# A decoder block on one core: earlier copies in the Entries, a reordered head, and attention keys split one step later

## The chip, the cores and the metric

One Trainium2 chip, one of its cores. The metric is the device time of one execution in microseconds; three runs of the kernel before are known, and one further execution was profiled.

## The reference

A hybrid decoder block on one sequence of 1024 tokens, model width 1024, in float32:

```python
h = x + 0.5 * swiglu(rms_norm(x, g1), w1a, w3a, w2a)           # swiglu: (silu(x@w1) * (x@w3)) @ w2, width 2816
u = rms_norm(h, g_mix)
q, k, v, p, gates = split(u @ w_in)                            # 768, 768, 768, 512, 2 x 1024 columns
y_attn = dilated_mixture_attention(q, k, v) @ w_branch_attn    # 3 groups of 4 heads, dilations 1, 4, 16, partial rotary
y_pool = multiscale_pool(p, pool_w, pool_scale) @ w_branch_pool
h = h + (sigmoid(gA) * y_attn + sigmoid(gB) * y_pool) @ w_out
h = h + 0.5 * swiglu(rms_norm(h, g2), w1b, w3b, w2b)
out = rms_norm(h, g_final)
```

## The kernel before, in words

Every large product is done in float32 by three matmuls of the format fp32r: each operand is split into an upper part (hi, a rounded copy made by ScalarE) and a lower part (lo, the operand minus hi, made by VectorE or GpSimd), and hi·hi, hi·lo and lo·hi are added up in PSUM. On top of that, products of 1024 x 1024 blocks go by a scheme of seven half-size products instead of eight (numbered 1 to 7, order 1, 6, 2, 7, 5, 4, 3), for which both operands need sums and differences of their quarters. TensorE, its weight loads, VectorE (DVE), ScalarE (ACT), GpSimd (POOL) and the DMA queues (most issued by SP, some by ACT) each work through their own queue in the order in which the program issues; most of that order is written out by hand (`manual_schedule`).

The stages, with the times in the profile at which they run:

- **Head** (0 to 28 us, `begin_up1`). Loads x and the gain, takes the squares and inverse roots of the first four row tiles (`squares` on ACT, `inverse` on DVE and then POOL), scales them, transposes them on TensorE (`Rows`) and makes their hi and lo. `keep_on` issues idle matmuls. The first four products (`entry.product(0)` to `(3)`) stand between.
- **Entry** (class `Entry`; three times: 28 to 60 us, 665 to 696 us, 1282 to 1315 us). While the first products of the stage run, it prepares the last four row tiles t = 4 to 7. Step t issues product i, three sets of transposes (y's high half for b22, all of it for t1 = its low half minus b11, and t3), product k = i + 1, and around them the sums t1, t2, t4 (on DVE, in PSUM), their hi on ACT, their lo on DVE, the weights two products ahead (`operand`: hi on ACT, lo on POOL or DVE), the outputs (`out`) and the scaling of the next tile. Product 2 of a quarter scheme accumulates in the bank of product 1, so it must wait until the output of product 1 has been copied out. `more` asks for the weights that the stage needs after the Entry; with `early` it only makes their sums s1 and s2 (`Quad.summed(6)`). `high(t, 0)` is `inverse(t)`, `high(t, 1)` the scaling, `after(t)` squares of tile t + 2 and loads. The four PSUM banks called "acc" are used in turn: the last transposes of step 7 take the bank that the lower part of t4 of step 6 has read last.
- **Up** (to 448 us, and from 1315 to 1713 us): the seven products for each pair of blocks of w1 and w3.
- **Down** (448 to 665 us, 1713 us to the end; class `Down`): steps of 24 matmuls; `begin(i + 2)` splits the operands of the step after next. Of the left operand's lower parts every second one goes to POOL in two halves, the others to DVE.
- **Mix** (696 to 1053 us): the input projection, with jobs between: rotations (`Mix.rotate`: y is stored, its rotary rows are gathered by DMA into a tile `ro`, turned, and stored), values transposed, pooling, late weights split. A job's `yield n` says that it goes on n products later.
- **Attention** (1053 to about 1180 us): 24 steps q of two slots of 128 queries each. Step q issues the scores of its slots, the transposes of the exponents of q - 1, branch products as filling, the values of q - 2, masks on DVE, and then on ACT the hi of the transposed exponents, the hi of the next head pair's keys and queries (`split_ring`, lo on POOL) and the exponents of step q.
- **Merge and output projection** (1180 to 1282 us): `merge(k)` on all engines, then 14 steps (`step_o`) of the seven-product scheme with left operands split by `split_o`; `rows_first2`, `lower` and `scaled2` prepare the second Entry between its last steps.

## Time and profile before

| | us |
|---|---|
| median of 3 runs | 1932.86 (1932.31 to 1933.2) |
| the profiled execution | 1933.69 |
| its span, first to last instruction | 1931.8 |
| TensorE busy (matmul) | 1900.9 |
| VectorE busy | 1341.1 |
| ScalarE busy | 776.9 |
| GpSimd busy | 732.4 |

Rows of the profile name the engine, the line of the kernel, the operation, and `out<-in` by the tiles' names (`u_f12a`: a product of the first up stage, pair 2, matrix a; `wc`: a split weight; `xhi`, `xlo`: parts of x; `alo`, `blo`: lower parts in a down stage; `tp`: transposed exponents). In a timeline the first number is the start in us, the second the duration, and square brackets tell how long the engine had been idle and what ended that. A matmul row counts as busy while it is in the pipeline, at a lowered clock too. The granted clock is given by the windows view as a share of full speed.

### The profile page before, as it was taken

Reading aid. Unit: us, or ns where it says so; the run is one execution under the profiler, and the core shown is the slowest. Engines: PE = TensorE matmul, PEld = TensorE weight load, DVE = VectorE, ACT = ScalarE, POOL = GpSimd, SP = SyncE. Lnnn points to the kernel's source line nnn. Section 1 sums busy time; section 2 is a strip of 40 time slices with the busy share of each in tenths; the row PEclk is TensorE's granted clock in tenths of the full one; section 3 lists DMA queues with packets and bytes.
Section 4 is the critical chain, followed back from the end, with each engine's and each line's share of the span. In section 5 each row is a group of like instructions: output and inputs, shape, how many; then the busy total and the mean of one; then the engine's idle time right before and its main releaser. Section 6 shows DMA issues by size and latency. Waiting matters only on the chain. (4 is left out here: it accounts for less than half of the span.)

```text
span 1931.8 us, 24861 instructions
## 1 busy us (share of the span) xinstructions
PE 1900.9 (98%) x8842; PEld 1567.5 (81%) x8842; DVE 1341.1 (69%) x2012; ACT 776.9 (40%) x1397; POOL 732.4 (38%) x559
## 2 busy tenths in 40 slices
PE   9999999999999999999999999999999999999998
PEld 7788888888888877888877888877888888888886
DVE  6786556658676776667775796877666556577777
ACT  6333333333345542334435663263323333333344
POOL 4333333332222344444545365543333333322133
PEclk9999999999999999999999999999999999999999
DMA  4154222336466637764568997643533223454564
GB/s 187 44 196 167 90 88 104 136 115 212 145 237 206 201 93 230 232 234 180 208 248 307 269 240 263 246 167 99 190 104 136 82 87 107 150 193 139 195 213 164
DMA packets 147436, 333.56 MB, mean 173 GB/s; under 512 B 20208, under 2 KB 40944, under 8 KB 145776
## 3 DMA queue, kind: packets, MB, share of 16 engines
q1 hardware_dynamic: 138096, 307.22, 47.1%
q10 hardware_dynamic: 9216, 24.75, 3.7%
q8 instruction: 70, 1.15, 0.2%
q14 instruction: 54, 0.44, 0.1%
HBM read 229.61 MB, written 102.30 MB: 172 GB/s over the span
## 5 line engine op out<-in xcount | busy, mean ns | idle before, releaser
L768 PE MATMUL d_f<-bhi_f,alo_f 128*128 128x512 f32 x616 | 240.4, 390 | 1.6 <-POOL alo_f L730 1.2
L768 PE MATMUL d_f<-bhi_f,ahi_f 128*128 128x512 f32 x616 | 240.6, 391 | 1.2 <-ACT ahi_f L726 0.7
L768 PE MATMUL d_f<-blo_f,ahi_f 128*128 128x512 f32 x616 | 239.8, 389 | 0.0
L730 POOL TENSOR_TENSOR alo_f<-g_f,ahi_f 128x512 fp32r<-128x512 f32 x68 | 96.9, 1442 | 278.6 <-ACT ahi_f L726 278.6
L314 PE MATMUL u_mixm<-xhi_t_mix,wc_mixm 128*128 128x512 f32 x608 | 195.2, 392 | 1.1 <-POOL wc_mixm L306 1.1
L314 PE MATMUL u_mixm<-xhi_b_mix,wc_mixm 128*128 128x512 f32 x456 | 148.8, 393 | 3.9 <-DVE y_m L1051 2.0
L768 PEld LDWEIGHTS d_f<-bhi_f,alo_f 128*128 128x128 f32 x616 | 115.6, 188 | 27.8 <-POOL alo_f L730 2.3
L768 PEld LDWEIGHTS d_f<-bhi_f,ahi_f 128*128 128x128 f32 x616 | 115.6, 188 | 25.6 <-ACT ahi_f L726 1.2
L314 PEld LDWEIGHTS u_mixm<-xhi_t_mix,wc_mixm 128*128 128x128 f32 x608 | 113.7, 188 | 26.4 <-POOL wc_mixm L306 3.0
L768 PEld LDWEIGHTS d_f<-blo_f,ahi_f 128*128 128x128 f32 x616 | 115.7, 188 | 23.9 <-DVE blo_f L730 0.2
L314 PE MATMUL u_mixm<-xlo_t_mix,wc_mixm 128*128 128x512 f32 x304 | 118.4, 389 | 0.0
L306 POOL TENSOR_TENSOR wc_mixm<-s_mixm,wc_mixm 128x512 fp32r<-128x512 f32 x52 | 75.2, 1447 | 102.8 <-ACT wc_mixm L303 87.9
L314 PEld LDWEIGHTS u_mixm<-xhi_b_mix,wc_mixm 128*128 128x128 f32 x456 | 85.6, 188 | 23.4 <-ACT late_hi L1194 2.6
L303 ACT ACTIVATE wc_mixm<-s_mixm 128x512 fp32r<-128x512 f32 x76 | 47.7, 629 | 124.8 <-DVE s_mixm L353 53.4
L314 PE MATMUL u_mixm<-xlo_b_mix,wc_mixm 128*128 128x512 f32 x228 | 88.8, 389 | 0.0
L726 ACT ACTIVATE ahi_f<-g_f 128x1024 fp32r<-128x1024 f32 x84 | 81.8, 974 | 3.0 <-DMA g_f<-gs_f 3.0
L306 POOL TENSOR_TENSOR wc_mixm<-raw,wc_mixm 128x512 fp32r<-128x512 f32 x40 | 56.5, 1414 | 59.1 <-ACT wc_mixm L303 56.5
L1958 PE MATMUL wo<-w_o,o_hi 128*128 128x512 f32 x224 | 69.5, 391 | 0.5 <-ACT h_again L395 0.3
L726 ACT ACTIVATE bhi_f<-s_f2w 128x512 fp32r<-128x512 f32 x55 | 32.9, 628 | 89.0 <-DVE s_f2w L746 81.3
L314 PEld LDWEIGHTS u_mixm<-xlo_t_mix,wc_mixm 128*128 128x128 f32 x304 | 57.1, 188 | 11.8
L726 ACT ACTIVATE bhi_f<-s_f1w 128x512 fp32r<-128x512 f32 x55 | 33.0, 630 | 79.4 <-DVE s_f1w L746 74.6
L730 DVE TENSOR_TENSOR alo_f<-g_f,ahi_f 128x1024 fp32r<-128x1024 f32 (+1 forms) x44 | 52.7, 1197 | 7.2 <-ACT ahi_f L726 7.2
(1332 smaller groups left out, 5099.8 us busy)
## 6 DMA issues: line engine op xcount, KB each, us to landing
g_f<-gs_f SPq DMA_DIRECT2D x70, 512.0 KB, 4.5
gs_f<-y_f SPq DMA_DIRECT2D x88, 256.0 KB, 2.5
raw<-in_w2a_dram SPq DMA_DIRECT2D x35, 512.0 KB, 3.9
raw<-in_w2b_dram SPq DMA_DIRECT2D x35, 512.0 KB, 4.1
gs_f<-gb_f SPq DMA_DIRECT2D x46, 256.0 KB, 2.3
raw<-in_w1a_dram SPq DMA_DIRECT2D x22, 512.0 KB, 4.7
raw<-in_w3a_dram SPq DMA_DIRECT2D x22, 512.0 KB, 5.8
raw<-in_w1b_dram SPq DMA_DIRECT2D x22, 512.0 KB, 4.6
```

The costliest lines, as they stand in the source:

```text
L303: ac.activation(w[:, 0], src, AF.Copy)
L306: eng.tensor_tensor(w[:, 1], src, w[:, 0].bitcast(F32), op=OP.subtract)
L314: pe.matmul(p, a, b, start=(start and k == 0 and q == 0), stop=(k == 3 and q == 2), skip_group_check=not start)
L726: ac.activation(hi[:, c], src, AF.Copy)
L730: eng.tensor_tensor(lo[:, d], src[:, o], hi[:, d].bitcast(F32), op=OP.subtract)
L768: pe.matmul(self.banks[m][t], l, r, start=(first and q == 0), stop=(last and q == 2))
L1958: pe.matmul(banks[m][t], l, r, start=(st == 0 and j == 0 and q == 0), stop=(st == 1 and j == 1 and q == 2))
```

## The change

It has these parts; nothing else of the kernel differs, and every engine does the same arithmetic, apart from what moves between engines.

- Entries: the output of product i is issued right behind the first upper part, and no longer behind all three; the squares of the tile after next (`after`) come before the fourth part; the inverse of a tile is issued at the end of the step two before it; the next tile is scaled before the weights of product k + 2 are split; of the weight sums, s1 is made in step 5 and s2 in step 6, and the weight they belong to is split behind the lower part of t4.
- Head: the identity is loaded first; the squares of tiles 1 to 3 are issued in a row, the four lower parts behind the four scalings; the high half of the gain is copied by ACT and no longer by DVE; product 0 goes by terms (4 x hi·hi, 4 x with w's lower part, 4 x with x's).
- Down stages: the lower part of the left operand of step 1 is made by DVE in one piece, not by POOL in two.
- Rotations: the gathering of the rotary rows is issued one product later, and one multiplication moves from POOL to DVE.
- Attention: the next head pair's keys and queries are split in steps 3 and 4 for the first use, not in steps 2 and 3.
- Output projection: the first left operand is split by halves, and `scaled2(3)` is issued behind the first two lower parts.

The diff:

```diff
@@ -294,6 +294,7 @@
         def __init__(self, name, X, fw, fs=None):
             self.name, self.X, self.fw, self.fs = name, X, fw, fs or fw
             self.n_lo = 0
+            self.by_term = False
 
         def half_tile(self, tag, n):
             return self.fs.tile([P, HALF], F32, tag=tag, bufs=4, name=f"{tag}_{self.name}{n}")
@@ -308,11 +309,13 @@
 
         def product(self, p, w, x, start=True):
             hi, lo = self.X[x]
-            for k in range(4):
+            order = [(k, q) for k in range(4) for q in range(3)]
+            if self.by_term:
+                order = [(k, q) for q in (0, 2, 1) for k in range(4)]
+            for n, (k, q) in enumerate(order):
                 r = slice(k * P, (k + 1) * P)
-                for q, (a, b) in enumerate(three((w[:, 0, r], w[:, 1, r]), (hi[:, k, :], lo[:, k, :]))):
-                    pe.matmul(p, a, b, start=(start and k == 0 and q == 0), stop=(k == 3 and q == 2),
-                              skip_group_check=not start)
+                a, b = three((w[:, 0, r], w[:, 1, r]), (hi[:, k, :], lo[:, k, :]))[q]
+                pe.matmul(p, a, b, start=(start and n == 0), stop=(n == 11), skip_group_check=not start)
 
     ORDER = (1, 6, 2, 7, 5, 4, 3)
 
@@ -323,6 +326,7 @@
             self.sv, self.n = sv, n
             self.a = []
             self.bank, self.w, self.src = {}, {}, {}
+            self.s1 = None
 
         def get(self):
             r = raws.get()
@@ -332,7 +336,7 @@
             self.summed(m)
             self.w[m] = self.sv.split(self.src.pop(m), f"{self.n}{m}", eng)
 
-        def summed(self, m):
+        def summed(self, m, whole=True):
             if m in self.src:
                 return
             if not self.a or (m not in (1, 2) and len(self.a) == 2):
@@ -347,8 +351,11 @@
             elif m == 4:
                 src = a22
             elif m == 6:
-                self.s1 = half_tile("s", f"{n}1")
-                ve.tensor_tensor(self.s1, a21, a22, op=OP.add)
+                if self.s1 is None:
+                    self.s1 = half_tile("s", f"{n}1")
+                    ve.tensor_tensor(self.s1, a21, a22, op=OP.add)
+                if not whole:
+                    return
                 self.s2 = half_tile("s", f"{n}2")
                 ve.tensor_tensor(self.s2, self.s1, a11, op=OP.subtract)
                 src = self.s2
@@ -451,11 +458,13 @@
                     ve.tensor_tensor(t2, t2, b21, op=OP.subtract)
                     return Parts(X, "t4", t2, t)
 
+                if t == 4:
+                    high(5, 0)
                 self.product(i)
                 if not last:
-                    high(t + 1, 0)
                     self.operand(i + 2)
                     s = Rows(X, "b22", y[:, HIGHS], t)
+                    self.out(i)
                 else:
                     r3 = Rows(X, "t3", t3, t)
                 p12 = bank("acc", f"x_b12_{t}")
@@ -469,18 +478,22 @@
                     t2 = bank("acc", f"x_t2_{t}")
                     s.lower()
                     r1.lower()
-                    self.out(i)
                     self.product(k)
+                    y, t3 = scaled_rows(t + 1)
                     self.operand(k + 2)
-                    y, t3 = scaled_rows(t + 1)
                     r2 = second()
                     r3.lower()
                     r2.lower()
                     self.out(k)
+                    after(t)
                     r4 = fourth()
+                    if t > 4:
+                        self.more(0, t - 4)
+                    r4.lower()
                     if t == NT - 2:
                         self.more(0)
-                    r4.lower()
+                    if t + 2 < NT:
+                        high(t + 2, 0)
                 else:
                     t2 = bank("acc", f"x_t2_{t}")
                     r2 = second()
@@ -497,9 +510,7 @@
                     s.lower()
                     r4.lower()
                     self.out(k)
-                after(t)
-                if t == NT - 3:
-                    self.more(0, True)
+                    after(t)
 
 
     class Pair:
@@ -718,7 +729,7 @@
             )
             self.n_lo += 1
             whole = len(srcs) == 1 and srcs[0].shape[1] > 1
-            eng = gp if self.n_lo % 4 == 0 and n < len(self.steps) - 2 else ve
+            eng = gp if self.n_lo % 4 == 0 and 1 < n < len(self.steps) - 2 else ve
             at = 0
             for src in srcs:
                 n = src.shape[1]
@@ -817,6 +828,7 @@
     warm = consts.tile([P, 1], F32, name="warm")
     cnt = consts.tile([P, 4, 16], F32, name="cnt")
     psc = consts.tile([P, 4], F32, name="psc")
+    nc.scalar.dma_start(ident, c_ident)
     nc.scalar.dma_start(gain1, ffn1_norm)
     ac.activation(warm, mhalf, AF.Silu)
 
@@ -836,7 +848,6 @@
     columns = columns_tile.rearrange("p (k c) -> p k c", k=KT)
 
     def load_all():
-        nc.scalar.dma_start(ident, c_ident)
         load_rows(0, 1, 2, 3)
         raws.depth = 2
         raws.load()
@@ -852,7 +863,7 @@
 
     def pre_run(sv, todo, first, low):
         return Entry(sv, [(*((q.A, m, q.a_out), (q.B, m, q.b_out))[k],) for q, m in todo for k in range(2)], low,
-                     lambda n, early=False: (first.A.summed if early else first.A.operand)((6, 7)[n]))
+                     lambda n, part=0: first.A.summed(6, part > 1) if part else first.A.operand((6, 7)[n]))
 
     def begin_up1():
 
@@ -890,30 +901,29 @@
         g = [gains(b) for b in range(2)]
         keep_on(2)
         ve.tensor_copy(gain_row[:, LOWS], g[0])
-        squares(1, square)
-        squares(2, square)
+        for t in range(1, 4):
+            squares(t, square)
         rows(0, "b11", LOWS)
         inverse(1)
         keep_on(2)
+        rows(1, "b11", LOWS)
         inverse(2)
-        squares(3, square)
-        rows(1, "b11", LOWS)
-        r[0].lower()
-        keep_on(3)
+        keep_on(2)
         rows(2, "b11", LOWS)
         inverse(3)
-        r[1].lower()
         keep_on(3)
         pairs = [Pair(sv1, j, sums, True, j == 2) for j in range(3)]
         entry = pre_run(sv1, [(q, m) for m in (1, 2) for q in pairs[:2]] + [(pairs[2], m) for m in (1, 2)],
                         pairs[0], h[:4])
         entry.operand(0)
         rows(3, "b11", LOWS, "mm")
-        r[2].lower()
         keep_on(2)
-        r[3].lower()
-        ve.tensor_copy(gain_row[:, HIGHS], g[1])
+        ac.activation(gain_row[:, HIGHS], g[1], AF.Copy)
+        for t in range(4):
+            r[t].lower()
+        sv1.by_term = True
         entry.product(0)
+        sv1.by_term = False
         entry.operand(1)
         for t in range(4):
             r[t].keep(h[t][:, LOWS])
@@ -1085,14 +1095,14 @@
                     nc.scalar.dma_start(given[:, a, n].rearrange("t r c -> r t c"),
                                         y[a][n * HD:n * HD + 16].rearrange("r (t c) -> r t c", t=2))
                 nc.scalar.dma_start(qk_dram[u][a].rearrange("h d c -> (h d) c"), y[a])
-                yield 1 + a
+                yield 1 + 2 * a
             ro = tmp(f"ro{u}").rearrange("p (a c) -> p a c", a=2)
             nc.scalar.dma_start(ro[:, 0, :], given.rearrange("t a h r c -> (t a h r) c"))
             yield 3
             tab = tables[g]
 
             ve.stream_shuffle(ro[:, 1, :], ro[:, 0, :], [i ^ 8 for i in range(32)])
-            gp.tensor_tensor(ro[:, 1, :], ro[:, 1, :], tab[:, 1, :], op=OP.mult)
+            ve.tensor_tensor(ro[:, 1, :], ro[:, 1, :], tab[:, 1, :], op=OP.mult)
             ve.tensor_tensor(ro[:, 0, :], ro[:, 0, :], tab[:, 0, :], op=OP.mult)
             if self.hp == 1 and g + 1 < GROUPS:
                 load_table(g + 1)
@@ -1264,13 +1274,13 @@
     mixes = [Mix(svm, q) for q in range(AHEAD)]
     items = [(q, m) for q in range(len(MIX)) for m in ORDER if q >= AHEAD or m not in (1, 2)]
 
-    def mix_operand(k, early=False):
+    def mix_operand(k, part=0):
         if k < len(items):
             q, m = items[k]
             if q == len(mixes):
                 mixes.append(Mix(svm, q))
-            if early:
-                mixes[q].quad.summed(m)
+            if part:
+                mixes[q].quad.summed(m, part > 1)
             else:
                 mixes[q].quad.operand(m, None if k > 1 else gp)
 
@@ -1845,9 +1855,12 @@
                 load_ring(uses[u + 1], ring_place(u + 1))
             if q > 0:
                 advance(splits[q - 1], 2)
-            if i > 1 and u + 1 < len(uses):
+            if i > 1 and 0 < u < len(uses) - 1:
                 split_ring(uses[u + 1], i - 2)
                 split_ring(uses[u + 1], i)
+            if q in (3, 4):
+                split_ring(uses[1], q - 3)
+                split_ring(uses[1], q - 1)
             end_branches()
             exponents(2 * q)
             exponents(2 * q + 1)
@@ -1936,8 +1949,11 @@
             for q in range(2):
                 gp.tensor_tensor(lefts[i][:, q], srcs[0][:, q], srcs[1][:, q], op=left[2])
 
+    def o_parts(i):
+        return tuple(op.tile([P, 2, HALF], F32R, tag=f"a{part}", bufs=3, name=f"o_{part}{i}") for part in ("hi", "lo"))
+
     def hi_o(i):
-        ops[i] = tuple(op.tile([P, 2, HALF], F32R, tag=f"a{part}", bufs=3, name=f"o_{part}{i}") for part in ("hi", "lo"))
+        ops[i] = o_parts(i)
         ac.activation(ops[i][0], lefts[i], AF.Copy)
 
     def lo_o(i):
@@ -1945,6 +1961,13 @@
         ve.tensor_tensor(lo, lefts.pop(i), hi.bitcast(F32), op=OP.subtract)
 
     def split_o(i):
+        if i == 0:
+            ops[i] = o_parts(i)
+            (hi, lo), src = ops[i], lefts.pop(i)
+            for q in range(2):
+                ac.activation(hi[:, q], src[:, q], AF.Copy)
+                ve.tensor_tensor(lo[:, q], src[:, q], hi[:, q].bitcast(F32), op=OP.subtract)
+            return
         hi_o(i)
         lo_o(i)
 
@@ -2044,7 +2067,6 @@
         scaled2(1)
         inverse(3)
         scaled2(2)
-        scaled2(3)
         step_o(STEPS - 4)
         raws.end = len(raws.pieces)
         raws.depth = 4
@@ -2052,6 +2074,7 @@
         r = [rows_first2(t) for t in range(2)]
         step_o(STEPS - 3, range(2))
         lower(0, r[0])
+        scaled2(3)
         lower(1, r[1])
         split_o(STEPS - 1)
         r.append(rows_first2(2))
```

## The prediction

> **What bounds the kernel now.** The page comes first: the span, and the share of each engine.
>
> ```profile
> span 1931.8 us, 24861 instructions
> ...
> PE 1900.9 (98%) x8842; PEld 1567.5 (81%) x8842; DVE 1341.1 (69%) x2012; ACT 776.9 (40%) x1397; POOL 732.4 (38%) x559
> ```
>
> TensorE is busy for 98% of the span, so nothing can be won by taking work off another engine as such. The change adds no matmul and removes none; it can only shorten TensorE's waits. The second view lists those waits by who ended them (microseconds in total, times, longest).
>
> ```profile
> PE tp L1630 <- ACT e L1610: 2.6, 2, 2.5
> PE u_f12a L314 <- ACT y_f L535: 2.3, 1, 2.3
> PE u_f21a L314 <- ACT y_f L535: 2.3, 1, 2.3
> PE u_mixm L314 <- DVE y_m L1051: 2.0, 3, 1.3
> PE u_mixm L314 <- ACT y_m L1040: 1.9, 1, 1.9
> PE d_f L768 <- POOL alo_f L730: 1.2, 2, 0.6
> PE x_b L387 <- DVE x L270: 1.1, 3, 0.6
> ...
> PE wo L1958 <- DVE o_lo L1945: 0.5, 1, 0.5
> ...
> PE u_f10a L314 <- DVE xlo_b_f L391: 0.2, 1, 0.2
> ```
>
> These rows come to 14.1 us. Rows 2, 3 and 5 are the three Entries, row 1 the start of attention, row 4 the mix stage beside a rotation, row 6 the two down stages, row 8 the first output step, rows 7 and 9 the head. Every edit aims at one of them. A wait can cost more than it lasts, which the third view shows: TensorE's busy time, then its granted clock, over windows of 3.41 us.
>
> ```profile
> 684.26:687.67 3.41, 1.86 (x9) 1.00 0.00 0
> 1066.55:1069.96 3.41, 0.90 (x10) 1.00 0.88 258
> 1302.07:1305.48 3.41, 1.06 (x5) 1.00 0.00 0
> 52.79:56.20 3.41, 3.41 (x9) 0.50 0.45 154
> 1069.96:1073.38 3.42, 3.42 (x13) 0.50 1.05 377
> 1305.48:1308.90 3.42, 3.42 (x9) 0.50 0.38 147
> ```
>
> After each of the three waits of over 2.3 us TensorE runs one stretch of 3.41 us at clock 0.50, counted as busy. It does half the work of that stretch, so each of these waits costs a further 3.41 / 2 = 1.71 us. The 1.9 us wait (first row, 45% idle) costs none; the two windows with 69 and 74% idle do. The Trainium skill (TensorE: Matmul & The Clock Gate, "What's actually happening") says the clock falls to half only after a whole idle window of about 3.4 us; by it none of these waits could do this, and the 5.1 us would not be among the gains. The trace agrees on the half clock and the window's length, but windows 69% idle are enough here, and I go by the trace.
>
> **The Entries.** Step t of an Entry does two products with three sets of transposes between; VectorE takes the sums and lower parts. In the second Entry (last: products of f21a and f21b), timeline rows of VectorE, ScalarE, TensorE:
>
> ```profile
> 1300.84 0.69 DVE L407 TENSOR_TENSOR xlo_t_f<-x_t,xhi_t_f 128x512 fp32r<-128x512 f32 x1 [0.66 <-ACT xhi_t_f L404]
> 1301.44 0.68 DVE L351 TENSOR_TENSOR s_f20a<-raw 128x512 f32<-128x512 f32 x1
> 1302.16 0.69 DVE L353 TENSOR_TENSOR s_f20a<-s_f20a,raw 128x512 f32<-128x512 f32 x1
> 1302.77 0.15 DVE L263 TENSOR_SCALAR nst<-nst 128x1 f32<-128x1 f32 x1
> ...
> 1309.95 0.69 DVE L306 TENSOR_TENSOR wc_f20a<-s_f20a,wc_f20a 128x512 fp32r<-128x512 f32 x1 [1.18 <-ACT wc_f20a L303]
> 1310.56 0.68 DVE L407 TENSOR_TENSOR xlo_t_f<-x_t,xhi_t_f 128x512 fp32r<-128x512 f32 x1
> ```
>
> ```profile
> 1301.22 0.59 ACT L388 ACTIVATE xhi_b_f<-x_b 128x512 fp32r<-128x512 f32 x1
> ...
> 1304.53 0.60 ACT L535 ACTIVATE y_f<-u_f21a 128x512 f32<-128x512 f32 x1
> ```
>
> ```profile
> 1305.18 0.56 PE L314 MATMUL u_f21a<-xhi_b_f,wc_f21a 128*128 128x512 f32 x1 [2.35 <-ACT y_f L535]
> ...
> 1311.30 0.66 PE L387 MATMUL x_b<-ident,hn_f 128*128 128x128 f32 x4 [0.63 <-DVE xlo_t_f L407]
> 1311.71 0.47 PE L314 MATMUL u_f21b<-xhi_b_f,wc_f21b 128*128 128x512 f32 x1
> ```
>
> The product at 1305.18 accumulates in the bank that the copy at 1304.53 must first read. That copy stands on ScalarE behind two upper parts, and one of these behind VectorE's queue with the two weight sums. The change puts the copy (out) right behind the upper part at 1301.22, which needs no sum: it then ends at about 1301.22 + 2 x 0.6 = 1302.4, before TensorE comes at 1305.18 - 2.35 = 1302.83. So the 2.35 us and, with it, the 1.71 us go.
>
> What is late next is VectorE. The last step's third set of transposes (1311.30) needs the bank freed by the lower part at 1310.56. On the path to it: the two weight sums, 1302.77 - 1301.44 = 1.33 us, now fill waits of 0.66 such as the one at 1300.84 (one a step earlier, one in step 6), and the weight's lower part at 1309.95 moves behind the lower part. Of its wait and pitch, 1.18 + 0.61 = 1.79 us, 0.66 stays as the wait for the upper part, so 1.1 us goes. The squares, moved ahead of the fourth part, free ScalarE sooner for the next step's first upper part, of which I count 0.3; the copy now stands ahead of t1's upper part and of VectorE's lower part that needs it, at most 0.6, of which I count 0.25. Sum 1.33 + 1.1 + 0.3 - 0.25 = 2.5 us; TensorE arrives sooner than that and waits about 2 us in two pieces in the last step. I take 2.4 (bounds 0, if the new waits bring the slow clock and a late operand, to 2.35 + 1.71 + 0.63 = 4.7).
>
> The first Entry has the same sums, but its weight's lower part is POOL's, so the 1.1 is missing: 1.33 + 0.3 - 0.25 = 1.4, more where the slow products had been the later of the two; with the head below, 2.0 (bounds 0.5 to 4.1). The mix Entry likewise: 1.4 (bounds 0.5 to 1.9 + 0.3). The weight loads that follow the squares on SP's queue go out with them, sooner and waited for by nobody here. On POOL the subtraction for t3 now stands ahead of the second weight's lower part; both are wanted within one product, which hides the later one (if not: up to 0.7 us in a step, in the bounds).
>
> **Head.** Squares in a row, lower parts all behind the four scalings, and the first product by terms: it needs its x lower parts only for its last four matmuls. Against that, each scaling now follows its own inverse through POOL, with no lower part between to fill VectorE, and ident's load, first on ScalarE's queue, puts gain1 one issue later. The two waits rows of the head hold 1.3 us; I take 0.3 (bounds -0.6 to 0.6), inside the 2.0 above.
>
> **Down stages.** Step 1's left lower part goes from POOL (two halves) to VectorE (one).
>
> ```profile
> 443.55 3.48 DVE L730 TENSOR_TENSOR blo_f<-s_f1w,bhi_f 128x512 fp32r<-128x512 f32 x2
> 446.95 1.21 DVE L730 TENSOR_TENSOR alo_f<-g_f,ahi_f 128x1024 fp32r<-128x1024 f32 x1
> ...
> 449.41 1.28 DVE L730 TENSOR_TENSOR blo_f<-s_f1w,bhi_f 128x512 fp32r<-128x512 f32 x2
> ```
>
> ```profile
> 443.08 3.39 POOL L730 TENSOR_TENSOR alo_f<-g_f,ahi_f 128x512 fp32r<-128x512 f32 x2 [2.90 <-ACT ahi_f L726]
> ```
>
> Beside POOL's 3.39 us the two VectorE ops take 3.48; alone, at 449.41, 1.28. Queued behind them are the pair's last outputs and step 2's sums. So 2.2 us is won and the new op costs 1.2: VectorE runs about 1.0 us ahead. The 0.6 us wait comes two steps later, at step 3, whose lower part stays on POOL; it is fed through VectorE's sums and shrinks by about 0.5, and step 0's own lower part, at 446.95, is sooner. Taken: 0.6 for each of two stages, 1.2 (bounds 0 to 1.5).
>
> **Rotations.**
>
> ```profile
> 731.13 1.78 DVE L351 TENSOR_TENSOR s_mixm<-raw 128x512 f32<-128x512 f32 x1
> ...
> 735.03 0.68 DVE L1051 TENSOR_TENSOR y_m<-u_mixm,y_m 128x512 f32<-128x512 f32 x1
> ```
>
> The 1.3 us wait ends with the op at 735.03, late because the shuffle, a multiplication and two weight sums stand before it, one of them stretched to 1.78 beside POOL's multiplication. One step later the shuffle and both multiplications stand behind it, and the reload on ScalarE's queue no longer holds up the engine until its own store has landed (a second of the three waits, all on L1051). 2.0 us is listed; I take 1.6 (bounds -1 to 2.0).
>
> **Attention.**
>
> ```profile
> 1068.07 0.63 ACT L1221 ACTIVATE xlo_b_mix<-xhi_b_mix 128x512 fp32r<-128x512 f32 x1 [2.10 <-DMA xhi_b_mix<-rot]
> ```
>
> ```profile
> 1068.78 1.27 POOL L1222 TENSOR_TENSOR xhi_b_mix<-xhi_b_mix,xlo_b_mix 128x512 fp32r<-128x512 f32 x1 [1.45 <-ACT xlo_b_mix L1221]
> ```
>
> ```profile
> 1069.25 2.17 PE L1630 MATMUL tp<-ident,e 128*128 128x128 f32 x8 [2.46 <-ACT e L1610]
> ...
> 1074.65 0.33 PE L1583 MATMUL s<-xlo_b_mix 64*128 64x128 f32 x2
> ```
>
> ```profile
> 1369.92 19.04 PE u_f22a L314 x84
> ```
>
> ScalarE stands in its queue for a load that lands at 1068.07, with the exponents behind it. A step later it does not. TensorE then goes on at 1069.25 - 2.46 = 1066.79 with 8 transposes (half of 2.17, which was at half clock), 4 matmuls (19.04 / 84 = 0.227 each, the last row, from the chain) and the values (12 of half that width, 1.4), and reaches the next scores, at 1074.65 now, at 1070.2. But these need the second lower part: ScalarE makes ehi from about 1067.4 and the ring's upper parts from 1068.6 (four copies of 0.6), POOL two lower parts of 1.27 from 1069.25, the second done at 1071.8. A new wait of about 1.4 us, too short for the slow clock: gain 1074.65 + 0.16 - 1071.85 = 2.9, taken as 2.7 (bounds 1.5 to 2.46 + 1.71 = 4.2).
>
> **Output steps.**
>
> ```profile
> 1187.51 0.50 PE L1958 MATMUL wo<-w_o,o_lo 128*128 128x512 f32 x1 [0.53 <-DVE o_lo L1945]
> ```
>
> By halves, the first lower part is ready before TensorE comes: the 0.53, a shorter wait just before it, and the restarts around both: 1.0 (bounds 0.5 to 1.2). On VectorE the second half waits for its upper part with the next merge's multiplication behind it, as the whole does now. scaled2(3), moved behind the first lowers, frees two banks sooner, but the next rows wait for copies queued behind an unmoved split: 0 (bounds -0.2 to 0.4).
>
> **Sum.** 2.0 + 1.4 + 2.4 + 1.2 + 1.6 + 2.7 + 1.0 = 12.3 us. The profiled execution took 1933.69, so 1921.4; the median of the three runs, 1932.86, is 0.83 below it, so 1920.6.
>
> **Rivals.**
> The slow clock stays in two Entries: the new waits there (about 2 us in one window of 3.41, 59% idle) lie between the 45% that did no harm and the 69% that did. 2 x 1.71 = 3.4 us back: 1924.0. Chance 0.20.
> The three slow stretches have another cause than the waits and stay: 3 x 1.71 = 5.1 us, 1925.7. All three follow the three longest waits, so 0.04. The Trainium skill's rule above would have it so.
> VectorE is no bound: the Entries' waits go whole, 4.1 + 1.9 + 4.7 instead of 5.8, 4.9 us more: 1915.7. Chance 0.10.
> Slower: VectorE's share of a rotation (a shuffle and two multiplications, of 0.7 us each like the sum at 1301.44, or up to 1.78 each beside POOL's other ops) now delays an output that a product waits for, six times. If each of the six costs over 12.3 / 6 = 2.05 us the change loses; at 2.35 + 1.71 = 4.06 us each it is 24.4 us, 1945.0. Against it: the trace shows one long wait of this kind among six rotations. Chance 0.07.
> The edits only move waits, and nothing is gained: 1932.9. Chance 0.03.
>
> **How the numbers follow.** The forecast has the remaining 0.56. The range 1915.5 to 1926.5 holds it and the first three rivals (0.90), with the bounds inside each. Faster 0.90, same 0.03, slower 0.07; 0.2%, 3.9 us, is about what a measurement of this kernel can tell from no change.
>
> **What would show it.** In the profile after: no wait of u_f12a, u_f21a and u_mixm for ACT y; a wait of x_b for xlo_t of 1 to 2 us in each Entry; a wait of s for POOL's ring of about 1.4 us near 1070; clock 1.00 throughout; no wait over 0.3 us for POOL alo_f at step 3; wo's first lower part without a wait. I am wrong if a window of an Entry shows clock 0.50, if rotations show waits over 2 us, or if the exponents still wait for the load.

## The result, and the profile after

The change makes the kernel faster: 1923.76 us median of 4 executions (1921.17 to 1925.59) beside 1933.03 before; the ratio is 0.9951, with a 95% interval of 0.9934 to 0.9968. The forecast was 1920.6, with a range of 1915.5 to 1926.5. The profiled execution of the changed kernel took 1924.18 us.

The page of the changed kernel, span and engines:

```profile
span 1922.4 us, 24860 instructions
...
PE 1896.7 (99%) x8840; PEld 1566.1 (81%) x8840; DVE 1337.6 (70%) x2020; ACT 777.4 (40%) x1399; POOL 715.8 (37%) x549
```

TensorE's work is the same; the span is 9.4 us shorter. The waits of TensorE by who ended them (microseconds in total, times, longest):

```profile
PE x_b L394 <- DVE xlo_t_f L414: 3.2, 2, 1.6
PE yp L1727 <- DMA wab<-late_w: 1.7, 1, 1.7
PE x_b L394 <- DVE xlo_t_mix L414: 1.6, 1, 1.6
...
PE wo L1981 <- ACT h_again L402: 1.0, 1, 1.0
...
PE wo L1981 <- DVE o_lo L1961: 0.8, 1, 0.8
...
PE d_f L779 <- POOL alo_f L741: 0.6, 2, 0.3
PE u_mixm L318 <- DVE y_m L1061: 0.6, 2, 0.3
```

All five long waits of before are gone: the copies of the three Entries, the exponents, and the 1.3 us one beside a rotation. Rows 1 and 3 are the forecast's wait of TensorE for VectorE, 1.6 us in the last step of each Entry. Row 2 was not forecast: attention now waits for a branch weight's load, where a wait for POOL's part of the keys had been expected. Rows 4 and 5 are the output stage, where the wait of 0.53 us shrank to 0.23 and longer ones came later.

The windows view (TensorE busy and its count, weight loads, VectorE, ScalarE, POOL, then the granted clock, DMA share, GB/s):

```profile
1297.21:1300.62 3.41, 1.73 (x13) 1.07 (x12) 3.23 (x6) 2.35 (x5) 1.74 (x2) 1.00 0.48 159
1300.62:1304.04 3.42, 3.42 (x11) 2.84 (x11) 3.35 (x6) 2.39 (x5) 0.00 (x0) 0.50 0.45 143
1061.69:1065.11 3.42, 1.76 (x11) 1.51 (x11) 2.10 (x8) 3.42 (x11) 1.98 (x2) 1.00 1.03 388
```

One stretch at clock 0.50 is left, where three were: it follows a window of the second Entry that was 49% idle (1 - 1.73 / 3.41). The third row, 49% idle too by the rounded numbers (1 - 1.76 / 3.42), has no slow stretch behind it.

Where the 9.4 us came from is read from the timeline of TensorE: the start of the first matmul of a stage, in both kernels, and the difference from one such start to the next (the head from the start of the span, the last stage to the end of its last matmul). For the second Entry and the products behind it, the timeline of the changed kernel:

```profile
1274.30 0.39 PE L318 MATMUL u_f20a<-xhi_b_f,wc_f20a 128*128 128x512 f32 x1
...
1703.23 0.39 PE L779 MATMUL d_f<-bhi_f,ahi_f 128*128 128x512 f32 x1
```

and of the kernel before:

```profile
1282.06 0.39 PE L314 MATMUL u_f20a<-xhi_b_f,wc_f20a 128*128 128x512 f32 x1
...
1712.48 0.39 PE L768 MATMUL d_f<-bhi_f,ahi_f 128*128 128x512 f32 x1
```

That is 428.93 against 430.42 us, 1.5 less. So for all stages, in the profiled executions:

| stage (from its first matmul to the next stage's) | before, us | after, us | gain | forecast |
|---|---|---|---|---|
| head, to the first transposes of t3 in the first Entry | 31.97 | 32.84 | -0.9 | 0.3 |
| first Entry and its products | 415.49 | 413.16 | 2.3 | 1.7 |
| first down stage | 217.89 | 216.86 | 1.0 | 0.6 |
| mix Entry, to its first product of t2 | 30.91 | 28.98 | 1.9 | 1.4 |
| rest of the mix stage, rotations | 356.86 | 355.26 | 1.6 | 1.6 |
| attention, to its last product of values | 118.15 | 116.06 | 2.1 | 2.7 |
| merge and output projection | 110.79 | 111.14 | -0.4 | 1.0 |
| second Entry and its products | 430.42 | 428.93 | 1.5 | 2.4 |
| second down stage | 212.64 | 212.47 | 0.2 | 0.6 |

The same table was made for each run below; it says more than the total, because some stages repeat within a few hundredths where no slow stretch (3.41 us at clock 0.50) falls and no load is late: the second Entry's stage took 427.55 to 427.59 us in seven kernels that have the changed Entry, or one that differs from it only in its last step, and no slow stretch in it. The head (31.97 to 32.70 with its old code), the rest of the mix stage (355.92 to 356.86) and the second down stage (212.46 to 212.82) scatter more, so one trace decides nothing there that is smaller. Attention took 117.15 to 118.87 us in the four kernels with its old code and no idle matmuls, a slow stretch in each.

### The profile page after: what moved, and what is told of

Same layout as the page of the kernel before. It is cut to its first block, busy times and chain, and to the rows that moved or that the text cites. A ratio compares the mean times of both kernels' runs of the same rounds, so it can differ in the third digit from the quotient of the medians.

```text
span 1922.4 us, 24860 instructions
## 1 busy us (share of the span) xinstructions
PE 1896.7 (99%) x8840; PEld 1566.1 (81%) x8840; DVE 1337.6 (70%) x2020; ACT 777.4 (40%) x1399; POOL 715.8 (37%) x549
## 5 line engine op out<-in xcount | busy, mean ns | idle before, releaser
L741 POOL TENSOR_TENSOR alo_f<-g_f,ahi_f 128x512 fp32r<-128x512 f32 x64 | 90.1, 1426 | 284.1 <-ACT ahi_f L737 275.8
```

What stands on the lines that cost most here:

```text
L741: eng.tensor_tensor(lo[:, d], src[:, o], hi[:, d].bitcast(F32), op=OP.subtract)
```

## The experiments

The theory was that VectorE's queue sets the end of each Entry, that half-idle windows bring the half clock, and that each part gains what its stage's next operand allows. Each run's before is the median beside which it was timed.

**Idle matmuls in the long waits of the kernel before.** Seven matmuls of ones go into a bank that is written next:

```diff
+                if last:
+                    b7 = bank("acc", f"x_t3_{t}")
+                    for _ in range(7):
+                        pe.matmul(b7[:, :P], ones, ones, start=True, stop=True)
                 self.product(i)
...
+        for _ in range(7 if q == 3 else 0):
+            pe.matmul(banks[0][:, :P], ones, ones, start=True, stop=True)
```

> The kernel before with seven matmuls of ones, whose result nobody reads, ahead of the last step's first product in each Entry and ahead of the transposes of the exponents of step 3 of attention, so that TensorE is busy in the three waits of over 2.3 us, which stay as long as they are. My theory (these waits bring the half clock): the three stretches at clock 0.50 vanish and nothing else changes, 3 x 1.71 = 5.1 us, 1932.9 - 5.1 = 1927.8. Rival (the slow stretches have another cause): they stay, no change, 1932.9. If idle matmuls themselves are late for the waiting operations: up to 0.3 us each slower.

Measured: 1935.79 (1934.25 to 1936.81), before 1933.41; ratio 1.0011 (1.0001 to 1.0020). The clock stayed at 1.00 in both Entries of its trace, so the waits do bring the half clock there. In the second Entry the idle matmuls waited 1.4 us for their own bank and filled the rest. In attention they ran too soon, the transposes waited 3.2 us behind them, and the slow stretch came twice: that stage took 121.53 us instead of 118.15, which is why the total rose. But the second Entry's stage and the mix Entry took the time they had (430.40 and 30.89 us), and the first Entry's only 0.5 less (415.00), with a head 0.7 longer. Neither theory had expected that. Its waits and its timeline around the second Entry:

```profile
PE x_b L387 <- DVE xlo_t_f L407: 2.1, 2, 1.6
```

```profile
1284.67 0.39 PE L314 MATMUL u_f20a<-xhi_b_f,wc_f20a 128*128 128x512 f32 x1
...
1715.07 0.39 PE L772 MATMUL d_f<-bhi_f,ahi_f 128*128 128x512 f32 x1
```

430.40 us, as before's 430.42. The idle matmuls start the product 0.6 us later, but at the full clock TensorE still comes 1.0 us sooner to the last transposes, and waits there for VectorE's lower part, 1.6 us instead of 0.6: they start 29.2 us after the stage's first matmul in both. In the kernel before, the slow stretch of this Entry was free.

**The copy alone.** In the kernel before, only `self.out(i)` is moved behind the first upper part:

```diff
                     s = Rows(X, "b22", y[:, HIGHS], t)
+                    self.out(i)
...
                     r1.lower()
-                    self.out(i)
                     self.product(k)
```

> The kernel before with one line of the change alone: the output of product i behind the first upper part in each Entry; weight sums, squares and inverses where they were. My theory (VectorE's queue is the next bound, and it is as full as before): the waits for the copy go and come back as waits of x_b for xlo_t in the last step, of 2 to 4.5 us, the slow clock with them; gain 0 to 2 us, 1931 to 1933. Rival (VectorE is no bound, the copy was all): 2.3 + 1.9 + 2.35 of waits and 2 x 1.71 of slow clock, 10 us, 1923.

Measured: 1935.14 (1932.23 to 1938.89), before 1933.41; ratio 1.0010 (1.0000 to 1.0019). Its waits:

```profile
PE x_b L387 <- DVE xlo_t_f L407: 2.3, 2, 1.7
...
PE u_f21a L314 <- POOL wc_f21a L306: 1.6, 1, 1.6
...
PE x_t L387 <- POOL s_f2t L436: 1.5, 2, 1.1
```

The 2.3 us waits for the copy are gone, no slow stretch falls into an Entry of this trace, and the second Entry's stage took 430.76 us. The wait turned up again for VectorE, as my theory had it, though shorter (1.7 us at most, not 2 to 4.5) and without the slow clock, and for POOL: its lower part of the weight stands behind an inverse that waited 3.6 us for VectorE, and its subtraction for t3 behind another weight's lower part. The copy that the profile of before named was not what set the time.

**The Entries' part alone**, all its lines on the kernel before (the diff's hunks for `summed`, `Entry.run` and `more`).

> The kernel before with the Entries' part of the change alone (copies, squares, inverses, weight sums; no head). My theory by the terms of the prediction: 1.7 + 1.4 + 2.4 = 5.5 us, 1927.4, with a wait of x_b for xlo_t of 1 to 2 us in each Entry. Rival (the slow clock stays in two Entries): 2.1 us, 1930.8. Rival (VectorE is no bound): 4.1 + 1.9 + 4.7 = 10.7 less the head's 0.6, 1922.8.

Measured: 1927.34 (1925.05 to 1929.79), before 1933.41; ratio 0.9970 (0.9958 to 0.9983), 6.1 us. By stages, without a slow stretch in an Entry: 2.3 us in the first Entry (415.49 to 413.15), 2.0 in the mix Entry (30.91 to 28.94), 2.9 in the second (430.42 to 427.55):

```profile
1276.47 0.39 PE L314 MATMUL u_f20a<-xhi_b_f,wc_f20a 128*128 128x512 f32 x1
...
1704.02 0.39 PE L776 MATMUL d_f<-bhi_f,ahi_f 128*128 128x512 f32 x1
```

So the copy alone does not pay, and the copy with the work that was moved beside it does. That this is the work on VectorE that was put into its waits, the two weight sums and the weight's lower part, is argued from the queues: no run moves them without the copy, or without the squares, the inverses and the scaling.

**The rotations alone**: `yield 1 + 2 * a`, and `gp` to `ve` in one multiplication, on the kernel before.

> The kernel before with the rotations' part alone: gathering one product later, one multiplication on VectorE. My theory: the 1.3 us wait and one of the two shorter ones on y_m go, 1.6 us, 1931.3. Rival (VectorE's larger share delays other outputs): no gain or slower, 1933 to 1945. Rival (the sum is only stretched by POOL, the place of the rotation does nothing): 1.1 us, 1931.8.

Measured: 1932.92 (1930.26 to 1934.21), before 1933.41; ratio 0.9994 (0.9985 to 1.0004). The total decides nothing. The rest of the mix stage took 355.45 us instead of 356.86, 1.4 less, and the wait of 1.3 us, which all five traces with the old code have, is gone. The other four took 355.92 to 356.53, so the gain lies between 0.5 and 1.4 by this trace.

**Attention alone**: `split_ring` for the first use in steps 3 and 4, on the kernel before.

> The kernel before with the attention part alone: the next keys split in steps 3 and 4. By the prediction's term: the 2.5 us wait and the slow clock go, a wait of up to 1.4 us for POOL's ring part or for the branch weight comes, 2.7 us, 1930.2 beside 1932.9. Rival (the wait for the branch weight, which the trace of the whole change shows in its place, brings the slow clock too in most runs): 1.0 us, 1931.9.

Measured: 1932.30 (1931.17 to 1934.31), before 1932.93; ratio 0.9999 (0.9989 to 1.0008). In its trace attention took 115.59 us instead of 118.15, 2.6 less, with a wait of 2.1 us in place of the old one. The total shows less than that: by its interval the change is between 2.1 us faster and 1.5 slower. The trace is of one of the faster executions (1931.26). What the others lost is not shown; the new wait may bring the slow stretch in them, as the rival had it, and in the trace it missed narrowly (a window 49.9% idle, at clock 1.00 behind it).

**Four parts undone in the changed kernel**: `ident` behind the gain again, the rotation's multiplication on POOL, step 1's left lower part on POOL, the first output operand whole.

```diff
-            eng = gp if self.n_lo % 4 == 0 and 1 < n < len(self.steps) - 2 else ve
+            eng = gp if self.n_lo % 4 == 0 and n < len(self.steps) - 2 else ve
...
-    nc.scalar.dma_start(ident, c_ident)
...
+        nc.scalar.dma_start(ident, c_ident)
...
-            ve.tensor_tensor(ro[:, 1, :], ro[:, 1, :], tab[:, 1, :], op=OP.mult)
+            gp.tensor_tensor(ro[:, 1, :], ro[:, 1, :], tab[:, 1, :], op=OP.mult)
...
-        if i == 0:
+        if i < 0:
             ops[i] = o_parts(i)
```

> The changed kernel with four small parts undone, each in a stage of its own, read from where TensorE stands at the stage's ends: ident loaded behind the gain again, the rotation's multiplication on POOL again, the left lower part of step 1 of the down stages on POOL again, the first output operand split whole again. By the terms of the prediction: head 0 to 0.6 sooner, rotations 0 to 0.5 later, down stages 2 x 0.6 later, output 1.0 later; together 1.5 to 2.5 us slower, 1925.3 to 1926.3 beside 1923.8. Rival (the traces of the whole change, which show 0.7 in the first down stage, nothing in the second, and a loss in the output stage): 0 to 1 us slower.

Measured: 1924.03 (1922.93 to 1925.94), before 1932.93; ratio 0.9957 (0.9942 to 0.9972), the changed kernel's time; but its trace has no slow stretch, and the changed kernel's has one. By stages: the head 32.74 us, within the scatter of both; the first down stage 217.78 instead of 216.86, 0.9 later; the second 212.54 instead of 212.47; the rest of the mix stage 356.27 instead of 355.26, 1.0 later. This last difference is no more than the stage scatters (the run with the last step put otherwise took 355.80 with VectorE's multiplication), so how much of the rotations' gain is the multiplication's stays open. What it does to VectorE is plain, first with POOL multiplying beside it (this run), then without (the changed kernel):

```profile
732.63 1.78 DVE L364 TENSOR_TENSOR s_mixm<-raw,raw 128x512 f32<-128x512 f32 x1
```

```profile
732.29 0.69 DVE L364 TENSOR_TENSOR s_mixm<-raw,raw 128x512 f32<-128x512 f32 x1
```

The output stage went the other way: 110.81 us whole, 111.14 by halves. All seven kernels that split the first operand whole took 110.79 to 110.83 there, all seven that split it by halves 110.88 to 111.31. By halves the first matmul with a lower part starts 1.2 us sooner in the stage (15.1 us after its start, not 16.25), and more than that is lost later, where the longer waits for o_lo and h_again stand.

**Two loads sooner** in the changed kernel:

```diff
-        load_ring(uses[1], ring_place(1))
         load_branch(1)
         load_gate(1)
+        load_ring(uses[1], ring_place(1))
...
-        for t in range(4, NT):
-            reload(t)
+            if k < 15:
+                reload(k - 7)
```

> The changed kernel with two loads issued sooner on SP's queue: the second branch weight and its gate ahead of the first use's ring in attention (the ring's load holds SP for 5 us until the last rotation is stored), and four tiles of h between the loads of the last merges, not behind all of them. My theory (these transfers replaced the waits that the change took away): the 1.66 us wait for wab goes and the wait for POOL's ring part that I forecast, up to 1.4 us, appears in part, gain 0.3 to 1.7; the wait of VectorE for h of 5.5 us shrinks, and the 0.8 us wait of wo for o_lo and the 1.05 us one for h_again with it, gain 0.5 to 1.5; together 1921.5 to 1923 beside 1923.8. Rival (the DMA engines are full there and the order of issue changes nothing): 1923.8.

Measured: 1925.91 (1921.11 to 1926.35), before 1932.93; ratio 0.9960 (0.9945 to 0.9975): no gain. Its waits:

```profile
PE s L1593 <- ACT xlo_b_mix L1231: 1.3, 1, 1.3
...
PE s L1593 <- POOL xhi_b_mix L1232: 1.0, 1, 1.0
```

The wait for the branch weight went, and the forecast's wait of the scores for the next keys took its place, of 2.3 us in two pieces and not 1.4, with a slow stretch behind it: attention took 117.67 us. The other load changed little: the output stage took 111.08, and VectorE waited for h for 5.3 us instead of 5.5. What holds that load back was not found. Part of this trace's time is not the edit's: a slow stretch in the first Entry (414.39 us, not 413.15), and a first down stage of 217.95 us. There VectorE waited longer than in the changed kernel for a transfer that its step 3 needs, and POOL's lower part behind it. VectorE's rows, the changed kernel's first, then this run's:

```profile
456.76 0.69 DVE L616 TENSOR_TENSOR gb_f<-y_f,y_f 128x512 f32<-128x512 f32 x1 [0.83 <-DMA gs_f<-gb_f]
```

```profile
458.60 0.69 DVE L616 TENSOR_TENSOR gb_f<-y_f,y_f 128x512 f32<-128x512 f32 x1 [1.93 <-DMA gs_f<-gb_f]
```

**The last step of each Entry put otherwise**: the transposes that are needed last go behind product k, and the first product after the Entry goes by terms.

```diff
                     r1 = Parts(X, "t1", p12, t)
-                    s = Rows(X, "b22", y[:, HIGHS], t)
...
                     self.product(k)
+                    self.sv.by_term = 1
+                    s = Rows(X, "b22", y[:, HIGHS], t)
```

> The changed kernel with the last step of each Entry put otherwise: the transposes of y's high half (needed last of all, by product 3) behind product k and not ahead of it, and the first product after the Entry by terms, so that it needs the lower part of t2 only for its last four matmuls. My theory (the 1.6 us waits of x_b come from the order of the transposes: product k has all it needs, and VectorE's next late operand is t2's, 1.1 us before the end of product k now): the three waits shrink by 1.1 us each, 3.3 us, and no window is half idle any more, 1.7 us for each slow stretch that is left: 1918 to 1920 beside 1923.8. Rival (VectorE's queue sets the end of the Entry whatever TensorE does): the wait turns up again ahead of the next product, gain under 0.5 us an Entry, 1922 to 1923.

Measured: 1922.04 (1921.56 to 1922.40), before 1932.93; ratio 0.9946 (0.9931 to 0.9960). The rival was right about the waits: they turned up again, as long as before, ahead of the next product. Waits, then timelines of TensorE, ScalarE and VectorE:

```profile
PE u_f20a L319 <- DVE xlo_t_f L399: 1.7, 1, 1.7
PE u_f10a L319 <- DVE xlo_t_f L399: 1.6, 1, 1.6
PE u_mixm L319 <- DVE xlo_t_mix L399: 1.6, 1, 1.6
```

```profile
1303.83 2.07 PE L319 MATMUL u_f20a<-xhi_t_f,wc_f20a 128*128 128x512 f32 x8 [1.71 <-DVE xlo_t_f L399]
```

```profile
1301.76 0.60 ACT L412 ACTIVATE xhi_t_f<-x_t 128x512 fp32r<-128x512 f32 x1 [0.88 <-DVE x_t L455]
```

```profile
1303.00 0.68 DVE L399 TENSOR_TENSOR xlo_t_f<-x_t,xhi_t_f 128x512 fp32r<-128x512 f32 x1
```

The product's operand was there at 1302.36; its bank was not, because VectorE's op at 1303.00 reads it. But idle time is now spread over more windows: the trace has no slow stretch at all, and the executions lie within 0.9 us, where those of the changed kernel lie within 4.4. (That did not last: those of the next run lie within 4.6.)

**That bank freed sooner**: as the run before, with `r3.lower()` right behind `second()`.

> As the run with the last step put otherwise, and besides VectorE makes t3's lower part right behind the sum for t2, not behind t2's lower part. In that run product 6 had its upper part at 1302.4 but waited until 1303.7 for the bank that t3's lower part reads last. My theory (that bank, one place in VectorE's order, is the whole wait): the bank is free at 1302.4, 1.3 us less in each of three Entries, no slow clock: 1922.0 - 3.9 = 1918.1. Rival (VectorE as a whole is too late and a later operand takes the place): under 0.4 us each, 1921 to 1922.

Measured: 1922.29 (1920.55 to 1925.16), before 1934.18; ratio 0.9941 (0.9929 to 0.9954). The product started sooner, and again it did not help: the second Entry's stage took 427.57 us, the first's 413.16. Waits came one operand on, for the weight of product 7, whose sum stands in VectorE's queue. Timelines of TensorE and VectorE:

```profile
1306.37 0.73 PE L319 MATMUL u_f20a<-xhi_t_f,wc_f20a 128*128 128x512 f32 x2 [0.63 <-POOL wc_f20a L307]
```

```profile
1303.55 0.68 DVE L365 TENSOR_TENSOR s_f20a<-raw,raw 128x512 f32<-128x512 f32 x1
```

**The scaling of tile 3 put back**, on that kernel.

> As the run before it in this list, and the scaling of tile 3 in the output stage where it stood before the change. My theory (this stage is set by VectorE's chain since the load of h landed, and the order inside it changes nothing): as the run before it within 0.3 us. Rival (the move costs 0.4 us: two waits of 0.31 and 0.32 became one of 1.05): 0.4 us faster.

Measured: 1923.88 (1920.70 to 1924.95), before 1934.18; ratio 0.9943 (0.9930 to 0.9955). The output stage took 111.09 us instead of 111.16: nothing, as forecast. The total is later because of attention (118.51 instead of 116.47), where the wait for the branch weight was 1.8 us and a slow stretch followed.

**Idle matmuls in the last step of the changed kernel**: six of them into the bank that `second` writes.

> The changed kernel with six matmuls of ones, whose result nobody reads, ahead of VectorE's sum for t2 in the last step of each Entry, so that TensorE is busy in the wait of 1.6 us ahead of the third set of transposes, which is as long as before. My theory (this wait brings the half clock in some executions of the changed kernel, by where the 3.41 us windows fall, and nothing hides it there): no slow stretch in an Entry, 1.4 us for each that went, median 1921 to 1922.3 beside 1923.8 and the runs closer together. Rival (VectorE hides the slow stretch, as in the kernel before with idle matmuls): 1923.8 with the same spread.

Measured: 1923.32 (1921.28 to 1924.90), before 1934.18; ratio 0.9942 (0.9929 to 0.9956). No Entry has a slow stretch; the second's stage took 427.57 us against 428.93 with one, so here it costs 1.36, and little hides it. But the median hardly moved and the executions still spread over 3.6 us. In the trace, attention waits longer than in any other, has the slow stretch behind it, and took 118.87 us:

```profile
PE yp L1729 <- DMA wab<-late_w: 3.9, 1, 3.9
```

**VectorE relieved**: as the run with the bank freed sooner, with the sum for product 7's weight on POOL and ahead of product k.

```diff
+                    self.sv.s7 = gp
+                    self.more(1)
+                    self.sv.s7 = ve
                     self.out(i)
                     self.product(k)
...
-                    self.more(1)
```

> As the run in which t3's lower part comes right behind the sum for t2, and besides the sum for the weight of product 7 is made by POOL, which stands idle for 6.7 us at the end of each Entry, and no longer by VectorE, and that weight is split one product sooner. There the wait that was left, 0.2 for ACT's and 0.6 us for POOL's part of this weight, stood behind VectorE's sum. My theory (VectorE's queue is what sets the end of an Entry, and taking an operation out of it, not moving TensorE's, is what gains): 0.8 us in each of three Entries, 2.4 us, 1919.9 beside 1922.3. Rival (the end is set elsewhere, by ScalarE's upper parts): under 0.3 us each, 1921.5 to 1922.3.

Measured: 1918.80 (1918.33 to 1919.71), before 1933.56; ratio 0.9926 (0.9913 to 0.9940). This version beats both kernels: its slowest execution is below the changed kernel's fastest. Against the run with the bank freed sooner, the first Entry's stage took 412.01 us instead of 413.16, the whole mix stage 383.10 instead of 383.44 (384.24 in the changed kernel), the second Entry's 427.27 instead of 427.57: 1.2, 0.3 and 0.3 us where 0.8 each were expected. So VectorE's queue was the bound in the first Entry. In the mix stage the wait of 0.6 us for that weight is gone too, but at a rotation TensorE then waits 0.6 us for VectorE. In the second Entry product 6 now waits for ScalarE's upper part of t2:

```profile
PE u_f20a L320 <- ACT xhi_t_f L413: 1.5, 1, 1.5
```

That is not ScalarE's doing: it had itself stood idle for VectorE. POOL's new sum ran beside VectorE's sum for the weight of product 6 and stretched it, from 0.68 us in the run with the bank freed sooner to 1.80. Timelines of POOL, VectorE and ScalarE:

```profile
1295.16 1.29 POOL L366 TENSOR_TENSOR s_f20a<-raw,raw 128x512 f32<-128x512 f32 x1
```

```profile
1295.20 1.80 DVE L362 TENSOR_TENSOR s_f20a<-s_f20a,raw 128x512 f32<-128x512 f32 x1
```

```profile
1299.10 0.60 ACT L413 ACTIVATE xhi_t_f<-x_t 128x512 fp32r<-128x512 f32 x1 [0.88 <-DVE x_t L456]
```

So VectorE is still the bound there, and what the move took out of its queue it gave back in this sum. The three stages make up 1.8 of the 3.1 us between the two traces; 1.4 are attention, 115.07 us beside 116.47, neither with a slow stretch, which this edit does not touch. That the executions lie within 1.4 us, though the wait for the branch weight is still 1.6 us in the trace, was not explained.

## Why the prediction was right or wrong

**The total.** The range held, and the sum of 12.3 us is nearly what the stages give where no slow stretch falls. From runs with and without each part: head -0.3 (mean 32.64 us with the new code, 32.33 with the old), first Entry 2.3, first down stage 1.0, mix Entry 1.9, rotations about 1.2 (mean 355.21 against 356.39), attention about 2.4 (mean 115.72 in six traces without a slow stretch, against 118.13 in the four with the old code), output -0.3, second Entry 2.9, second down stage about 0.5 (mean 212.08 against 212.62), together 11.6. The one execution with a mean clock of 1.000 took 1921.17, beside the forecast's 1920.6. That the sum comes so close is in part luck: the three Entries gave 7.1 us where 5.5 were counted, head and output -0.6 where 1.3 were.

**The step that failed: "too short for the slow clock".** The forecast took new waits of 1.4 to 2 us as harmless and the clock as 1.00 throughout, and named a window of an Entry at 0.50 as what would prove it wrong. The profiled execution has one. The limit lies near half a window, so it hangs on where the windows fall, and three of the four executions have a mean clock of 0.998. The median of 1923.76 is the first rival's 1924.0, which had a chance of 0.20, but it is not quite its mechanism: beside the Entries' 1.6 us waits it is attention's wait for the branch weight, 1.6 to 3.9 us in the traces. By the Trainium skill (TensorE: Matmul & The Clock Gate, "What's actually happening") only a wholly idle window would do this; the trace disagrees, with its window 49% idle.

**A slow stretch costs 1.71 us.** That was the size before anything hides it. In the second Entry it cost 0.0 before, under VectorE's queue, and 1.36 after, when VectorE was less late; in the first, about 0.5 before (415.49 beside 415.00) and 1.2 after (414.39 beside 413.15). The sum did not fail by this, because it counted what VectorE allows and not what TensorE's waits promise.

**VectorE is next.** Right: the copy alone gained nothing, the whole part 2.3, 2.0 and 2.9 us where 1.7, 1.4 and 2.4 were counted. The terms were about 0.5 us small in each Entry, and which of them is not shown. The 1.7 itself is 0.3 more than its terms add up to (1.33 + 0.3 - 0.25 = 1.4), with no row for the difference.

**Rotations.** Right within the scatter, 1.6 forecast and about 1.2 seen. The slower rival (six outputs each late by over 2 us) has nothing in the trace: no wait for y_m is over 0.3 us.

**Down stages.** 0.6 each were forecast; the first gave 1.0, the second about 0.5 within its scatter. The wait at step 3 was 0.5 to 0.7 us in all 14 stages with the old part, and is 0.4 or less in 12 of the 14 with the new one. In the other two VectorE waited 1.5 and 1.9 us for the transfer into gs_f, not 0.7 to 1.1, and TensorE's wait is 0.7 as before: a step that the forecast did not have.

**Attention.** 2.7 forecast; the six traces with the new split and no slow stretch took 115.07 to 116.47 us, 1.7 to 3.1 less than before. Three more have a slow stretch behind the new wait and took 117.67 to 118.87, so there the gain is nearly or wholly gone; the forecast called this wait too short for that. It was put down to POOL; in the changed kernel it is the load of the branch weight, which stands in SP's queue behind the keys' load, and POOL's comes when that load goes first.

**Output.** Wrong: 1.0 forecast, -0.3 measured. The first product's lower part did come sooner by 1.2 us, but nothing was left of that at the end of the stage. The forecast named no next operand there, as it had for the Entries.

**Head.** 0.3 forecast, about -0.3 seen, less than its scatter; the place of ident's load does not explain it.

## What to carry to other kernels

A wait names the operand that was last, not the one that would be last next: taking the copy away gained nothing, and two more changes of order in the last step only moved the wait. In the first Entry it took an operation out of the full engine's queue; in the second the engine that got the operation slowed the full one down. When an operation changes engines, look at what runs beside it there. Compare runs stage by stage from fixed instructions; totals with slow stretches in some executions and not in others hide effects of 1 us. Waits that fill about half a clock window are to be avoided for their scatter, even where their time alone seems small.

## What was not expected of the hardware

In the 14 traces of this case, taking TensorE's idle share of each 3.41 us window (one less its busy time over 3.41) on the grid that the clock records give: all 13 windows that were 52 to 94% idle were followed by a window at clock 0.50; of the seven with 48.6 to 50.0% three were (49.0, 49.3 and 49.5) and four were not; none under 48% was, but for one that was itself at half clock (34% idle). A wait of 2.3 us that fell across two windows (44% idle) did no harm, and one of 1.9 us that fell into one (55%) did. Seven idle matmuls kept the clock at 1.00 in an Entry without gaining time, since the half clock ran while VectorE was late anyway. VectorE's sum of 0.69 us takes 1.78 beside a multiplication on POOL, and 1.80 beside a sum on POOL. With that multiplication on VectorE the stage was 1.0 us shorter in one pair of traces, though VectorE has more to do; this is within what the stage scatters.
